# Hybrid flow step, one core: the first loads in another order, six conditioning units in the output projection, gates ahead of the first features

## The chip, the cores and the metric

The kernel runs on one core of one Trainium2 chip. What counts is the device time of one execution in microseconds (us). Engines are named as the profile names them: PE (matmul), PEld (weight load), DVE (vector), ACT (scalar), POOL (GpSimd), SP (the queue that issues all DMAs of this kernel).

## The reference, cut to what matters

640 tokens (512 latent, 128 context) of 1024 channels go through two layers. Each layer is scaled, shifted and gated by six vectors that come from the conditioning vectors `c` and `c_ctx`:

```python
mod_ctx = silu(c_ctx) @ w_mod[l] + b_mod[l]          # (6 * 1024)
mod_lat = silu(c) @ w_mod[l] + b_mod[l]
sh1, sc1, g1, sh2, sc2, g2 = split(mod, 6)
h = rmsnorm(x, ln1) * (1 + sc1) + sh1
a_qkv, a_z, a_beta, a_alpha, b_q, b_k, b_v, c_q, c_k, c_v, gates = split_cols(h @ w_in)
ya = gated_delta_net(conv_silu(a_qkv), sigmoid(a_beta), softplus(a_alpha), ...)   # mixer A
yb, yc = global_attention(...), window_attention(...)                             # mixers B, C
merged = sig(ga) * (ya @ w_br_a) + sig(gb) * (yb @ w_br_b) + sig(gc) * (yc @ w_br_c)
x = x + g1 * (merged @ w_o)                           # output projection
h2 = rmsnorm(x, ln2) * (1 + sc2) + sh2
x = x + g2 * (relu(h2 @ w_ff1) ** 2 @ w_ff2)
```

## The kernel before, in words

Data lie with channels on the 128 partitions and tokens along the row; the 640 tokens are worked on in two halves of 320. Every product of 32-bit numbers is made as three products of a rounded part (`hi`) and a rest (`lo`).

**Conditioning units.** `w_mod` of a layer is cut into 12 units of 512 columns (2 MB of weights each). Units 0 and 1 give `sh1`, 2 and 3 `sc1`, 4 and 5 `g1`, 6 and 7 `sh2`, 8 and 9 `sc2`, 10 and 11 `g2`. For layer 0 `mod_unit` (L248) makes a unit on PE with the raw 32-bit weights:

```python
for k0 in range(0, KC, nk):
    raw = (pl or fl).tile([P, nk, 512], F32, name="fraw", tag="fraw", bufs=bufs)
    nc.sync.dma_start(out=raw, in_=d["w_mod"][l, :, u, k0:k0 + nk])
    for k in range(k0, k0 + nk):
        for i in range(4):
            PE.matmul(ps[32 * i:32 * i + 32], lhsT=csil[:, 2 * k:2 * k + 32], rhs=raw[:, k - k0, i * P:(i + 1) * P], ...)
mod_finish(l, u, ps)
```

`mod_finish` copies the sums (ACT, L235), turns them with one PE transpose (L237), adds `b_mod` (DVE, L239), and for units 2, 3, 8, 9 makes the norm's scale `A` (DVE, L243). Units 0 to 3 run at the start with six buffers of 512 KB (two k each). The others run with eight loads of 256 KB and three buffers (`FR = 3`), which they share with the weights of the filling work. Layer 1's units are made on DVE during the MLP of layer 0 (`mod_sum`); the change leaves them.

**Norm and projection.** `norm` (L282) squares `x` on ACT, adds on DVE (L293), sums over partitions with small matmuls (L298), takes the power -0.5 on POOL, spreads it with small matmuls (L306), and then makes for each of eight k `x * A * rstd` (DVE, L312), plus `sh` (ACT, L314, tile `hh`) and the rest (DVE, L315).

**Mixer A and the filling work.** The projections of mixers B and C and of the branch gates are 36 units (`unit`, L412, matmuls L422) of 48 matmuls. They are recorded at low priority, and a scheduler places them between the instructions of mixer A (gated DeltaNet, "GDN") and of the attention. Mixer A's features are made by `gdn_feat` (L387: matmuls L189, convolution on DVE L405); its per-token gates (L440 to L514) from a projection with 32 matmuls (L451), a copy, a chain of small DVE and ACT instructions, and small matmuls (L490 to L493). `gdn_prep` (L518) transposes the features (L528), normalises them (DVE L542), transposes again (L546) and multiplies by the decay made from the gates (L556 to L561). Conditioning units 4 to 7 stand in the list of the filling work, one behind every eighth unit (`MS = 8`). Filling matmuls are also paced by SP (L201).

**Output projection** (L1115 to L1130, matmuls L189 on `mh`/`ml` and `ghi`/`glo`): eight column blocks j for the first half of the tokens, then eight for the second; `resid` adds to `x`. Units 8 to 11 are recorded behind blocks 0, 2, 4, 6 of the first half. Then the norm's second half and the MLP (L1132 on).

**Order.** Each engine works through its instructions in the order that the scheduler fixed when the program was built. A DMA waits on SP for its buffer, and also until the DMA eight before it has landed: the framework gives the DMAs eight completion semaphores in turn.

Of the kernel before, what the change touches and what calls it, by code (L numbers as in the profile page):

```python
# [9 lines left out]
F32 = mybir.dt.float32  # L10
# [7 lines left out]
P = 128  # L18
# [3 lines left out]
HALF = 320  # L22
DEPTH = 2
DFF = 4096
KC = 8
# [5 lines left out]
M_GDN, M_BND, M_N = 0, 192, 448  # L31
# [39 lines left out]
def weave(*gens):  # L71
    active = list(gens)
    while active:
        live = False
        for g in list(active):
            try:
                live |= next(g) is None
            except StopIteration:
                active.remove(g)
        if not live:  # L80
            return
# [3 lines left out]
MB, FM, FB, FR, OFF = 3, 2, 2, 3, 30000  # L85
PACE, PG = 4, 2
HK = (2, 4, 5)
MS, MP = 8, 0
WRING = 6


# [1 line left out]
def kernel(ctx: ExitStack, tc: tile.TileContext, d: dict):  # L93
    nc = tc.nc
    PE, ACT, DVE, POOL = nc.tensor, nc.scalar, nc.vector, nc.gpsimd

    def pool(name, side="left", bufs=1):
        return tc.tile_pool(name=name, bufs=bufs, side=side, reuse_waits="tile")

    cp = ctx.enter_context(tc.tile_pool(name="cp", bufs=1))  # L100
    psum, turn = {}, {}

    def psum_open(key, name, side, **tags):
        stk = ExitStack()
        pl = stk.enter_context(tc.tile_pool(name=name, bufs=1, space=bass.MemoryType.PSUM, side=side,
                                            reuse_waits="tile"))
        psum[key] = (stk, pl, tags)

    def psum_close(*keys):
        for k in keys:  # L110
            psum.pop(k)[0].close()

    def psum_phase(name, **tags):
        psum_close(*[k for k in ("main",) if k in psum])
        psum_open("main", name, "left", **tags)
# [6 lines left out]
    def bank(shape, tag="m", dt=F32):  # L122
        use = [v for v in psum.values() if tag in v[2]]
        turn[tag] = turn.get(tag, 0) + 1
        _, pl, tags = use[turn[tag] % len(use)]
        return pl.tile(shape, dt, name=tag, tag=tag, bufs=tags[tag])
# [5 lines left out]
    MUL, ADD, SUB = ALU.mult, ALU.add, ALU.subtract  # L132


    cst = cp.tile([P, C_N], F32, name="cst")
    nc.sync.dma_start(out=cst, in_=d["cst"])
    ident = cst[:, C_ID:C_ID + P]
# [13 lines left out]
    hx = ctx.enter_context(pool("hx", "left"))  # L151
    istk = ExitStack()
    npool = istk.enter_context(pool("in0", "left"))
    mraw = npool.tile([P, M_N], F32, name="mraw")
    nc.sync.dma_start(out=mraw, in_=d["msk"])
    mskb = cp.tile([P, 3, 64], BF16, name="mskb")
    DVE.tensor_copy(mskb, mraw[:, M_GDN:M_GDN + 192].rearrange("p (d i) -> p d i", d=3))
    bandb = cp.tile([P, 2, P], BF16, name="bandb")
    DVE.tensor_copy(bandb, mraw[:, M_BND:M_BND + 256].rearrange("p (d i) -> p d i", d=2))
    ones1 = cp.tile([P, 1], F32, name="ones1")  # L160
    DVE.memset(ones1, 1.0)
    mhalf = cp.tile([P, 16], F32, name="mhalf")
# [7 lines left out]
    def load_w(src, pl, bufs, tag="w", rb=2, lo_eng=None):  # L170
        shape = [P, src.shape[1], src.shape[2]]
        raw = pl.tile(shape, F32, name=tag + "raw", tag=tag + "raw", bufs=rb)
        hi = pl.tile(shape, F32R, name=tag + "hi", tag=tag + "hi", bufs=bufs)
        lo = pl.tile(shape, F32R, name=tag + "lo", tag=tag + "lo", bufs=bufs)
        nc.sync.dma_start(out=raw, in_=src)
        split(hi, lo, raw, lo_eng or POOL)
        return hi, lo

    def wcols(w, n, a=0, b=P):
        return [w[0][:, k, a:b] for k in range(n)], [w[1][:, k, a:b] for k in range(n)]  # L180
# [28 lines left out]
        ACT.activation(out, in_, AF.Tanh, scale=0.5)  # L209


    cc = cp.tile([P, KC, 2], F32, name="cc")
    nc.sync.dma_start(out=cc, in_=d["cc"])
    cth = cp.tile([P, KC, 2], F32, name="cth")
    tanh_half(cth, cc)
    csil = cp.tile([P, 2 * KC + 30], F32, name="csil")
# [15 lines left out]
    def mod_finish(l, u, ps):  # L232
        L = lay[l]
        sb = fl.tile([P, P], F32, name="modsb", tag="modsb", bufs=1)
        ACT.copy(sb, ps)  # L235
        pt = bank([P, 4, 32], "fm")
        PE.transpose(pt.rearrange("p i r -> p (i r)"), sb, ident)  # L237
        s = slice(4 * u, 4 * u + 4)
        tt(out=L["mod"][:, s], in0=pt[:, :, 0:2], in1=bc(L["b_mod"][:, s], 2, 2), op=ADD)  # L239
        for n, o in ((0, 8), (1, 32)):  # L240
            if o <= 4 * u < o + 8:
                ks = slice(4 * u - o, 4 * u - o + 4)
                stt(out=L["A"][:, n, ks], in0=L["mod"][:, s], scalar=1.0, in1=bc(L["ln"][:, n, ks], 2, 2),  # L243
                    op0=ADD, op1=MUL)
        if 16 <= 4 * u < 24:
            ts(out=L["g1h"][:, 4 * u - 16:4 * u - 12], in0=L["mod"][:, s], scalar1=0.5, scalar2=None, op0=MUL)

    def mod_unit(l, u, pl=None, nk=1, bufs=FR):  # L248
        ps = bank([P, P], "fm")
# [5 lines that stand above are left out]
                    PE.matmul(ps[32 * i:32 * i + 32], lhsT=csil[:, 2 * k:2 * k + 32], rhs=raw[:, k - k0, i * P:(i + 1) * P],  # L255
                              start=(k == 0), stop=(k == KC - 1), tile_position=(0, 32 * i))
        mod_finish(l, u, ps)
# [64 lines left out]
    xpool = ExitStack()  # L322
    xp = xpool.enter_context(pool("xp0", "right"))
    x = xp.tile([P, KC, NT], F32, name="x")
    for half in range(2):
        s = slice(half * HALF, half * HALF + HALF)
        nc.sync.dma_start(out=x[:, :, s], in_=d["xT"][:, :, s])

    def load_params(l, names):
        shapes = {"b_mod": [P, 48], "ln": [P, 2, KC], "rows": [P, R_N], "conv": [P, 12, 5], "an": [P, 1]}  # L330
        for n in names:
            lay[l][n] = cp.tile(shapes[n], F32, name=f"{n}{l}", tag=n, bufs=1 if n == "rows" else 2)
            nc.sync.dma_start(out=lay[l][n], in_=d[n][l])
# [6 lines left out]
    for l in range(DEPTH):  # L340
        L = lay[l]
        if l == 0:
            load_params(0, ("b_mod", "ln", "rows", "conv", "an"))
            load_params(1, ("b_mod", "ln"))
            psum_phase("ps_in", gm=4)
            for u in range(4):
                mod_unit(0, u, npool, 2, 6)
            istk.close()
        mods = [(mod_unit, l, u) for u in range(4, 8)] if l == 0 else []
        with tc.high_priority(offset=-OFF):  # L350
            for f, *a in mods[:MP]:
                f(*a)
# [23 lines left out]
        def gtile(shape, tag, dt=F32):  # L376
            return (gp if tag in G_EARLY else gdl).tile(shape, dt, name=tag, tag=tag, bufs=GB.get(tag, 1))
# [9 lines left out]
        def gdn_feat(hp, sk):  # L387
            for i in range(3):
                cb = gtile([P, 646], "cb")
                for a, b in ((0, 2), (514, 516), (644, 646)):  # L390
                    POOL.memset(cb[:, a:b], 0.0)
                w = wcols(load_w(d["w_fm"][l, hp * 3 + i], gp, WB), KC)
                for half in range(2):
                    ps = gemm_fm(w, hh, hl, half, TF)
                    if half == 0:
                        ACT.copy(cb[:, 2:322], ps)
                    else:
                        ACT.copy(cb[:, 322:514], ps[:, 0:192])
                        ACT.copy(cb[:, 516:644], ps[:, 192:320])
                yield  # L400
                acc = sk[:, i]
                ci = (4 + hp, hp, 8 + hp)[i]
                ACT.mul(acc, cb[:, 0:642], L["conv"][:, ci, 0:1])
                for j in range(1, 5):
                    stt(out=acc, in0=cb[:, j:j + 642], scalar=L["conv"][:, ci, j:j + 1], in1=acc, op0=MUL, op1=ADD)  # L405
                yield
                th = gtile([P, 642], "so")
                tanh_half(th, acc)
                stt(out=acc, in0=th, scalar=1.0, in1=acc, op0=ADD, op1=MUL)
                yield  # L410
# [23 lines left out]
        fills = [(unit, u) for u in U_ORDER + tuple(range(12, 36))]  # L434
        fills = [f for i in range(36) for f in fills[i:i + 1] + mods[i // MS:i // MS + 1] * (i % MS == MS - 1)]

        sk = gtile([P, 3, 642], "sk")
        weave(gdn_feat(0, sk))

        ba = gtile([P, 5, 32], "ba")  # L440
        wraw = gtile([P, KC, 32], "wraw")
        wba = gtile([P, KC, 2, 32], "whi", F32R)
# [3 lines left out]
        for half in range(2):  # L446
            s = slice(half * HALF, half * HALF + HALF)
# [65 lines left out]
        egs = gtile([P, 2, 5, 8], "egs")  # L513
        ACT.activation(egs.rearrange("p c t h -> p c (t h)"), gs, AF.Exp)  # L514

        cnt, busy, dbusy = [0, 0], {}, {}

        def gdn_prep(hp, t, sk, stg, out):  # L518
# [290 lines left out]
        for hp in range(3):  # L809
            nprep, ndab, nz = {}, [], {}  # L810
            sk = gtile([P, 3, 642], "sk")
# [287 lines left out]
        x = xp.tile([P, KC, NT], F32, name="x")  # L1099
# [17 lines left out]
        nrm = norm(l, 1, 0, x, h2h, h2l, sc)  # L1117
        for j in range(KC):
            resid(j, 0, gemm_fm(ws[j], mh, ml, 0), L["g1h"])
            if l == 0 and j in (0, 2, 4, 6):  # L1120
                mod_unit(0, {0: 8, 2: 9, 4: 10, 6: 11}[j])
        again = KC - WRING
        order = [*range(again, KC), *range(again)]
        for i, j in enumerate(order):
# [7 lines left out]
        with pool(f"ff{l}", "left") as fp:  # L1132
            mods = [(1, u) for u in range(12)] if l == 0 else []
# [165 lines left out]
    for half in range(2):  # L1299
        s = slice(half * HALF, half * HALF + HALF)  # L1300
# [104 lines left out]
```

## Time and profile before

| what | value |
|---|---|
| time, median of 3 runs (lowest, highest) | 2769.16 us (2767.98, 2770.24) |
| profiled execution: its time, its span | 2765.79 us, 2764.0 us |
| PE busy | 2631.6 us (95%) |
| DVE busy | 1989.5 us (72%) |
| ACT busy, POOL busy | 1262.2 us (46%), 977.6 us (35%) |
| DMA share, mean rate | 29.6% of 16 engines, 97 GB/s |

The span runs from the first to the last instruction that the profiler saw; the time of the same execution is 1.79 us longer. Busy time of PE counts matmuls that overlap their neighbours' ends, so a busy PE may still run at the lower of its two clock levels; the granted clock ("PEclk") is a column of its own.

### The profile page before, as it was taken

The page shows a single profiled execution, that of the slowest core. Times are in us where ns is not written, and L with a number is a line of the kernel's source. Part 1 is how long each engine was busy: PE and PEld are TensorE (multiplying, and loading weights), DVE is VectorE, ACT ScalarE, POOL GpSimd, SP SyncE. Part 2 cuts the span into 40 slices and gives each one's busy share as a digit, 9 for nine tenths or more (in the row PEclk, how much of TensorE's full clock was granted, in tenths as well). Part 3 has the DMA queues.
Part 4 walks back from the last instruction along what each step waited for, and adds up shares of the span by engine and source line. Part 5 has one row for each costly group of instructions (what it writes and reads, how often), then busy time and mean ns, then how long its engine had stood idle before and what let it go on. Part 6 is the DMA issues. An engine that isn't in the chain of part 4 may idle for free. (4 is left out here: it accounts for less than half of the span.)

```text
span 2764.0 us, 55264 instructions
## 1 busy us (share of the span) xinstructions
PE 2631.6 (95%) x20820; PEld 2454.3 (89%) x20820; DVE 1989.5 (72%) x4245; ACT 1262.2 (46%) x3054; POOL 977.6 (35%) x1269
## 2 busy tenths in 40 slices
PE   6989999999999999999999999999999999999999
PEld 4878888998888899999988888889998789999999
DVE  4788887555567478999966888875556676676564
ACT  3435545555544243444344355455555444343341
POOL 2534543463454011122125445444645530121110
PEclk8999999999999999999999999999999999999999
DMA  6231112232325523555422211112323241222221
GB/s 228 74 100 43 58 48 71 96 123 93 97 88 189 185 80 109 152 156 154 148 82 86 76 53 53 56 45 97 103 70 114 76 162 62 72 90 70 70 99 61
DMA packets 117017, 268.60 MB, mean 97 GB/s; under 512 B 13584, under 2 KB 22416, under 8 KB 116752
## 3 DMA queue, kind: packets, MB, share of 16 engines
q1 hardware_dynamic: 116752, 265.08, 29.6%
q8 instruction: 165, 2.70, 0.4%
q14 instruction: 100, 0.82, 0.1%
HBM read 232.52 MB, written 32.51 MB: 96 GB/s over the span
## 5 line engine op out<-in xcount | busy, mean ns | idle before, releaser
L422 PE MATMUL fm<-hh,fhi 128*128 128x320 f32 x2304 | 445.3, 325 | 18.9 <-ACT hh L314 8.3
L422 PEld LDWEIGHTS fm<-hh,fhi 128*128 128x128 f32 x2304 | 359.7, 194 | 32.2 <-ACT hh L314 11.3
L168 POOL TENSOR_TENSOR rl<-fr,rh 128x320 fp32r<-128x320 f32 x128 | 142.1, 1115 | 673.5 <-ACT rh L167 673.5
L168 POOL TENSOR_TENSOR flo<-fraw,fhi 128x512 fp32r<-128x512 f32 x176 | 240.0, 1365 | 248.2 <-ACT fhi L167 155.2
L167 ACT CAST ghi<-graw 128x1024 fp32r<-128x1024 f32 (+1 forms) x148 | 144.9, 980 | 225.5 <-PE gm L1259 129.9
L422 PE MATMUL fm<-hh,flo 128*128 128x320 f32 x1152 | 235.4, 324 | 9.2 <-SPq L201 9.1
L1106 DVE SCALAR_TENSOR_TENSOR x<-gm,mod,x 128x320 f32<-128x320 f32 (+2 forms) x384 | 153.9, 431 | 83.9 <-PE gm L1259 83.0
L168 DVE TENSOR_TENSOR glo<-graw,ghi 128x1024 fp32r<-128x1024 f32 (+1 forms) x148 | 171.5, 1160 | 35.7 <-ACT ghi L167 20.2
L1259 PE MATMUL gm<-rl,ghi 128*128 128x320 f32 x1024 | 196.6, 310 | 0.0
L1259 PE MATMUL gm<-rh,ghi 128*128 128x320 f32 x1024 | 195.1, 310 | 1.3 <-DVE x L1106 1.3
L422 PEld LDWEIGHTS fm<-hh,flo 128*128 128x128 f32 x1152 | 181.6, 193 | 16.6 <-SPq L201 10.4
L1259 PE MATMUL gm<-rh,glo 128*128 128x320 f32 x1024 | 192.0, 309 | 0.0
L167 ACT CAST fhi<-fraw 128x512 fp32r<-128x512 f32 x192 | 119.1, 620 | 148.8 <-PE fm L422 62.9
L189 PE MATMUL mb<-hh,whi 128*128 128x320 f32 x1024 | 169.9, 313 | 4.4 <-ACT whi L167 4.4
L1259 PEld LDWEIGHTS gm<-rh,ghi 128*128 128x128 f32 x1024 | 161.0, 188 | 2.7 <-issue 2.4
L1259 PEld LDWEIGHTS gm<-rl,ghi 128*128 128x128 f32 x1024 | 161.7, 188 | 1.0 <-issue 1.0
L1259 PEld LDWEIGHTS gm<-rh,glo 128*128 128x128 f32 x1024 | 160.8, 188 | 0.0
L189 PEld LDWEIGHTS mb<-hh,whi 128*128 128x128 f32 x1024 | 152.8, 188 | 7.3 <-ACT whi L167 5.3
L597 DVE TENSOR_TENSOR stmp<-sv 128x31 f32<-128x31 f32 (+15 forms) x248 | 131.0, 528 | 6.1
L270 DVE SCALAR_TENSOR_TENSOR macc<-fraw,csil,macc 128x512 f32<-128x512 f32 x168 | 133.9, 814 | 0.0
L1197 PE MATMUL gm<-hh,ghi 128*128 128x320 f32 x768 | 130.2, 310 | 0.0
L977 ACT ACTIVATE p<-s,nb 128x640 f32<-128x640 f32 (+3 forms) x160 | 103.0, 648 | 51.2 <-PE pt L1007 24.9
(330 smaller groups left out, 6325.2 us busy)
## 6 DMA issues: line engine op xcount, KB each, us to landing
graw<-w_ff SPq DMA_DIRECT2D x128, 512.0 KB, 3.3
fraw<-w_mod SPq DMA_DIRECT2D x160, 256.0 KB, 2.9
fraw<-w_fm SPq DMA_DIRECT2D x144, 256.0 KB, 2.8
f_spill<-fgt SPq DMA_DIRECT2D x72, 320.0 KB, 2.2
wraw<-w_fm SPq DMA_DIRECT2D x32, 512.0 KB, 3.4
gts<-f_spill SPq DMA_DIRECT2D x48, 320.0 KB, 3.1
fraw<-w_br SPq DMA_DIRECT2D x48, 256.0 KB, 2.8
graw<-w_o SPq DMA_DIRECT2D x20, 512.0 KB, 4.7
```

The costliest lines, as they stand in the source:

```text
L167: ACT.copy(hi, src)
L168: (lo_eng or DVE).tensor_tensor(out=lo, in0=src, in1=hi.bitcast(F32), op=SUB)
L189: mm = PE.matmul(ps, lhsT=w_[k], rhs=x_[:, k, s], start=(i == 0 and k == 0), stop=(i == 2 and k == n - 1))
L270: stt(out=a, in0=raw, scalar=c, in1=a, op0=MUL, op1=ADD)
L422: mm = PE.matmul(ps[half], lhsT=w[:, k], rhs=x_[:, 4 * q + k, s], start=(q == 0 and k == 0 and w is hi and x_ is hh), stop=(q == 1 and k = ...
L597: tt(out=tv, in0=bc(W[:, s + 1:32, s], 2, m), in1=bc(XX[:, s, 0:m], 1, n), op=MUL)
L977: ACT.activation(pw, pv, AF.Exp, bias=nb[:, h:h + 1], scale=0.125, accum_out=den[:, h:h + 1])
L1106: stt(out=x[:, j, a:b], in0=ps[:, a - t0:b - t0], scalar=gate[:, j, c:c + 1], in1=x[:, j, a:b], op0=MUL, op1=ADD)
L1197: PE.matmul(ps, lhsT=w_[:, 4 * q + k], rhs=x_[o][:, k], start=(first and i == 0 and k == 0), stop=(i == 2 and k == 3), skip_group_check=True)
L1259: PE.matmul(ps, lhsT=w_[k], rhs=r[k // 2][o][:, k % 2, half_of(half)], start=(i == 0 and k == 0), stop=(i == 2 and k == 3))
```

## The change

Five edits, and all line numbers behind them move up by one to four:

```
-MS, MP = 8, 0
+MS, MP = 14, 0
...
+    cc = cp.tile([P, KC, 2], F32, name="cc")
+    nc.sync.dma_start(out=cc, in_=d["cc"])
     cst = cp.tile([P, C_N], F32, name="cst")
     nc.sync.dma_start(out=cst, in_=d["cst"])
...
-    for half in range(2):
-        s = slice(half * HALF, half * HALF + HALF)
-        nc.sync.dma_start(out=x[:, :, s], in_=d["xT"][:, :, s])
...
         if l == 0:
-            load_params(0, ("b_mod", "ln", "rows", "conv", "an"))
-            load_params(1, ("b_mod", "ln"))
             psum_phase("ps_in", gm=4)
+            load_params(0, ("b_mod", "ln"))
             for u in range(4):
                 mod_unit(0, u, npool, 2, 6)
+                if u < 2:
+                    s = slice(u * HALF, u * HALF + HALF)
+                    nc.sync.dma_start(out=x[:, :, s], in_=d["xT"][:, :, s])
+            load_params(0, ("rows", "conv", "an"))
+            load_params(1, ("b_mod", "ln"))
+            mraw = npool.tile([P, M_N], F32, name="mraw")
+            nc.sync.dma_start(out=mraw, in_=d["msk"])
+            DVE.tensor_copy(mskb, mraw[:, M_GDN:M_GDN + 192].rearrange("p (d i) -> p d i", d=3))
+            DVE.tensor_copy(bandb, mraw[:, M_BND:M_BND + 256].rearrange("p (d i) -> p d i", d=2))
             istk.close()
-        mods = [(mod_unit, l, u) for u in range(4, 8)] if l == 0 else []
+        mods = [(mod_unit, l, u) for u in range(4, 6)] if l == 0 else []
...
-        sk = gtile([P, 3, 642], "sk")
-        weave(gdn_feat(0, sk))
...
+        sk = gtile([P, 3, 642], "sk")
+        weave(gdn_feat(0, sk))
...
             resid(j, 0, gemm_fm(ws[j], mh, ml, 0), L["g1h"])
-            if l == 0 and j in (0, 2, 4, 6):
-                mod_unit(0, {0: 8, 2: 9, 4: 10, 6: 11}[j])
+            if l == 0 and j in (0, 1, 2, 3, 4, 5):
+                mod_unit(0, {0: 6, 1: 7, 2: 8, 3: 9, 4: 10, 5: 11}[j])
```

The number of PE matmuls in the built program is the same, 17,706. Where they stand differs; three places follow. A row is an instruction or a run of equal ones; in the changed kernel `mod_unit`'s load and matmul are L248 and L251, its transpose L233, the norm's matmuls L294 and L302, `gemm_fm`'s L187, the gates' L448, L453 and L487 on.

SP, the program's first rows, before: (`fraw<-w_mod` is a load of a conditioning unit, `xT` the input, `msk` the masks, the rest parameters)

```order
L136 DMA cst<-cst 128x740
L155 DMA mraw<-msk 128x448
L213 DMA cc<-cc 128x16
L327 DMA x<-xT 128x8x320 x2
L333 DMA b_mod_118<-b_mod 128x48
L333 DMA ln_120<-ln 128x16
L333 DMA rows_122<-rows 128x296
L333 DMA conv_124<-conv 128x60
L333 DMA an_126<-an 128x1
L333 DMA b_mod_128<-b_mod 128x48
L333 DMA ln_130<-ln 128x16
L252 DMA fraw<-w_mod 128x1024 x6
```

and of the changed kernel:

```order
L136 DMA cc<-cc 128x16
L138 DMA cst<-cst 128x740
L325 DMA b_mod_115<-b_mod 128x48
L325 DMA ln_117<-ln 128x16
L248 DMA fraw<-w_mod 128x1024 x4
L341 DMA x<-xT 128x8x320
L248 DMA fraw<-w_mod 128x1024 x2
L341 DMA x<-xT 128x8x320
L248 DMA fraw<-w_mod 128x1024
L325 DMA rows_307<-rows 128x296
L325 DMA conv_309<-conv 128x60
L248 DMA fraw<-w_mod 128x1024
```

The first weight is the fifth load instead of the thirteenth; seven small loads and the masks' load stand among the weights of units 1 and 2 (the fence ends in them).

PE, around the gates of layer 0, before: (`mb` on L189 are features, `fm` on L422 filling work, L451 and L456 the gates' projection and its transposes, L528 `gdn_prep`)

```order
L189 MATMUL mb<-hh,whi 128x320
L189 MATMUL mb<-hh,wlo 128x320 x8
L422 MATMUL fm<-hh,flo 128x320
L422 MATMUL fm<-hh,fhi 128x320 x4
L451 MATMUL mb<-hh,whi 64x320 x32
L528 MATMUL mb<-cst,sk 128x128 x2
L422 MATMUL fm<-hh,fhi 128x320 x4
L422 MATMUL fm<-hh,flo 128x320
L456 MATMUL ma<-cst,zz 128x32 x2
```

and of the changed kernel:

```order
L422 MATMUL fm<-hh,fhi 128x320 x8
L448 MATMUL mb<-hh,whi 64x320 x32
L422 MATMUL fm<-hh,flo 128x320 x4
L422 MATMUL fm<-hh,fhi 128x320 x3
L453 MATMUL ma<-cst,zz 128x32 x2
L422 MATMUL fm<-hh,fhi 128x320
L453 MATMUL ma<-cst,zz 128x32 x3
L422 MATMUL fm<-hh,fhi 128x320 x4
L187 MATMUL mb<-hh,whi 128x320 x28
```

The gates' 32 matmuls stand in the second filling unit, behind its first eight matmuls and ahead of the first feature matmul, instead of behind the last feature.

PE, the end of the output projection's second half and the norm behind it, before: (`hh` at the end is the MLP's first block)

```order
L189 MATMUL gm<-mh,glo 128x320 x8
L298 MATMUL gm<-ones_85,nacc 64x1
L298 MATMUL gm<-ones_85,nacc 128x1 x2
L306 MATMUL gm<-cst,nrstd 128x64
L306 MATMUL gm<-cst,nrstd 128x128 x2
L189 MATMUL gm<-hh,ghi 128x320 x16
```

and of the changed kernel:

```order
L187 MATMUL gm<-mh,glo 128x320 x8
L233 MATMUL fm<-cst,modsb 128x128
L251 MATMUL fm<-fraw,csil 32x128 x16
L294 MATMUL gm<-ones_83,nacc 64x1
L294 MATMUL gm<-ones_83,nacc 128x1 x2
L251 MATMUL fm<-fraw,csil 32x128 x8
L302 MATMUL gm<-cst,nrstd 128x64
L302 MATMUL gm<-cst,nrstd 128x128 x2
L187 MATMUL gm<-hh,ghi 128x320 x16
```

Six of the last unit's eight groups of four matmuls stand between the last block and the norm's two small products.

## Rows read from the trace of the kernel before

**Rows 1.** The page's first part: busy us (share of the span) and instructions.

```profile
PE 2631.6 (95%) x20820; PEld 2454.3 (89%) x20820; DVE 1989.5 (72%) x4245; ACT 1262.2 (46%) x3054; POOL 977.6 (35%) x1269
```

**Rows 2.** Timeline of SP from the start: start us, us, engine, line, transfer.

```profile
2.11 1.37 SPq L327 DMA_DIRECT2D x<-xT  x2
...
13.05 2.89 SPq L252 DMA_DIRECT2D fraw<-w_mod  x6
```

**Rows 3.** Waits of SP in 0 to 60 us: total us, times, longest.

```profile
SPq L252 <- DMA x<-xT: 3.3, 1, 3.3
```

**Rows 4.** Windows: stretch, length, busy us by engine, PEclk, DMA share, GB/s.

```profile
2.00:12.00 10.00, 0.00 (x0) 0.00 (x0) 2.62 (x10) 2.39 (x7) 0.00 (x0) 1.00 0.99 329
12.00:14.00 2.00, 0.00 (x0) 0.00 (x0) 1.56 (x4) 1.84 (x5) 0.00 (x0) 1.00 0.42 83
14.00:22.00 8.00, 6.38 (x56) 5.05 (x60) 3.87 (x11) 2.99 (x7) 1.04 (x1) 1.00 1.01 383
22.00:24.00 2.00, 2.00 (x34) 1.31 (x26) 0.28 (x3) 0.00 (x0) 0.39 (x1) 1.00 0.57 163
24.00:40.00 16.00, 11.53 (x170) 8.01 (x169) 1.49 (x6) 2.27 (x6) 2.97 (x3) 0.78 1.02 400
```

**Rows 5.** Timeline of DVE, 38 to 60 us.

```profile
38.98 0.17 DVE L243 SCALAR_TENSOR_TENSOR A<-mod,ln 128x8 f32<-128x8 f32 x1
...
43.91 0.17 DVE L243 SCALAR_TENSOR_TENSOR A<-mod,ln 128x8 f32<-128x8 f32 x1
...
57.80 1.03 DVE L315 SCALAR_TENSOR_TENSOR hh<-ntmp,mod,hh 128x128 fp32r<-128x128 f32 x3
```

**Rows 6.** Waits of PE in 150 to 200, 400 to 450 and 540 to 700 us.

```profile
PE fm L255 <- DMA fraw<-w_mod: 3.4, 3, 1.6
...
PE fm L255 <- DMA fraw<-w_mod: 1.8, 1, 1.8
...
PE fm L255 <- DMA fraw<-w_mod: 2.8, 5, 1.2
```

**Rows 7.** Windows around units 4 to 7, the end of attention, the output projection.

```profile
190.00:204.00 14.00, 10.63 (x111) 8.13 (x110) 5.99 (x9) 6.08 (x18) 5.03 (x18) 0.88 0.57 180
424.00:442.00 18.00, 16.20 (x173) 11.68 (x173) 11.96 (x35) 9.37 (x32) 7.70 (x14) 0.81 0.53 156
556.00:570.00 14.00, 12.58 (x141) 9.85 (x140) 4.37 (x10) 5.56 (x17) 9.16 (x13) 0.76 0.65 209
670.00:684.00 14.00, 12.63 (x153) 9.42 (x152) 8.80 (x19) 6.68 (x17) 8.23 (x13) 1.00 0.67 207
900.00:966.00 66.00, 66.00 (x597) 56.10 (x596) 29.09 (x61) 18.14 (x33) 4.98 (x5) 1.00 0.57 180
...
856.00:868.00 12.00, 9.44 (x93) 6.78 (x92) 9.23 (x36) 6.60 (x25) 3.28 (x6) 1.00 0.23 67
```

**Rows 8.** The loads of L252 in 880 to 966 us: issue to landing.

```profile
DMA to landing us min/median/max: 2.6/3.1/5.7
```

**Rows 9.** Timeline of PE in the output projection: a unit's matmuls, three runs of blocks'.

```profile
908.71 0.64 PE L255 MATMUL fm<-fraw,csil 128*32 128x128 f32 x16
909.28 0.71 PE L189 MATMUL gm<-mh,ghi 128*128 128x320 f32 x3
909.83 1.33 PE L189 MATMUL gm<-ml,ghi 128*128 128x320 f32 x8
911.00 1.33 PE L189 MATMUL gm<-mh,glo 128*128 128x320 f32 x8
```

**Rows 10.** Waits of PE in 840 to 1010 us.

```profile
PE gm L298 <- DVE nacc L293: 2.9, 1, 2.9
...
PE gm L306 <- POOL nrstd L206: 1.3, 1, 1.3
```

**Rows 11.** Waits of PE in 100 to 130 us, then in 1480 to 1530 us.

```profile
PE mb L546 <- DVE tm L542: 2.5, 2, 1.4
...
PE mb L546 <- DVE tm L542: 2.6, 2, 1.6
```

More of the change, by code (lines that the diff above doesn't have):

```diff
@@ L153 @@
     npool = istk.enter_context(pool("in0", "left"))
-    mraw = npool.tile([P, M_N], F32, name="mraw")
-    nc.sync.dma_start(out=mraw, in_=d["msk"])
     mskb = cp.tile([P, 3, 64], BF16, name="mskb")
-    DVE.tensor_copy(mskb, mraw[:, M_GDN:M_GDN + 192].rearrange("p (d i) -> p d i", d=3))
     bandb = cp.tile([P, 2, P], BF16, name="bandb")
-    DVE.tensor_copy(bandb, mraw[:, M_BND:M_BND + 256].rearrange("p (d i) -> p d i", d=2))
     ones1 = cp.tile([P, 1], F32, name="ones1")
@@ L209, in tanh_half @@
         ACT.activation(out, in_, AF.Tanh, scale=0.5)
-    cc = cp.tile([P, KC, 2], F32, name="cc")
-    nc.sync.dma_start(out=cc, in_=d["cc"])
     cth = cp.tile([P, KC, 2], F32, name="cth")
```

## The prediction, made blind

> **What bounds the kernel now.** I read the page's first part: PE is busy for 2631.6 of 2764.0 us, every other engine for far less [rows 1]. The program has 17,706 matmuls before and after, so the change can only move time in which PE waits, or in which PE works at the lower clock. I therefore went through the stretches that the change touches: SP's timeline and waits at the start, with the rate of the DMAs; PE's waits and granted clock around each conditioning unit that stands in the filling work; the output projection; PE's waits on mixer A's gates. In each the reader is to see what PE waits for, and for how long.
>
> At the start PE waits for the stream of loads. `x` is issued at 2.11 us, but the first weight of a conditioning unit only at 13.05 us [rows 2], held for 3.3 us by `x` [rows 3], since the DMA eight before it must have landed. The windows show the hole that this leaves: 12 to 14 us runs at a share of 0.42, and 22 to 24 us at 0.57; between them the DMAs are full, at 329 GB/s while `x` comes and at 400 GB/s later on weights [rows 4]. The last unit's scale `A` is made at 43.91 us; behind it DVE makes the norm's rows without a break, until 57.80 + 1.03 = 58.83 us [rows 5]. Only then has PE more work than it can do. So the start costs the end of the stream plus a fixed DVE chain of 14.75 us.
>
> The sum is made against the profiled execution: 2764.0 us of span and 1.79 around it, 2765.79 us. The median of the runs is 3.37 us above that; I add this to the end.
>
> **The first loads, -4.3 us (bounds -6.2 and -1.7).** From 2 to 40 us the DMAs moved 3.29 + 0.17 + 3.06 + 0.33 + 6.40 = 13.25 MB [rows 4]. In the new order two loads of `w_fm` (0.26 MB each, from their shape) fall behind the last unit's weights, so 12.73 MB precede its end. The weights now start with the fifth load and nothing but their own buffers and the loads eight before hold them, so the two holes should close. With 3.29 MB at 329 GB/s (10 us) and the other 9.44 MB at 400 (23.6 us) the stream ends at 2 + 33.6 = 35.6 us instead of 40: -4.4, less a tenth for the small loads. All at 400 would end at 33.8: -6.2. If both holes come back (2 x 0.58 + 2 x 0.43 = 2.0 us) and one `w_fm` comes ahead after all (0.6), -1.7 is left; these two are the bounds. The casts of the masks on DVE now wait for a load behind units 1 and 2, ahead of the second half's norm sum; they land some 10 us before unit 2's `A`, so they cost nothing unless the stream is late there (this is in the lower bound).
>
> **Two units out of the filling work, -8.2 us (bounds -10.3 and -4.0).** Units 4 to 7 made PE wait 3.4, 1.8 and (two together) 2.8 us for their weights, 8.0 in all [rows 6]; that is 2.0 for a unit. Around three of them the granted clock falls below 1: 0.88 over 14 us, 0.81 over 18, 0.76 over 14, and 1.00 around the fourth [rows 7]. Length times what is missing from 1: 1.7 + 3.4 + 3.4 + 0 = 8.5 us lost, 2.1 for a unit. Two units stay in the filling work, behind the 14th and the 28th filling unit, and two leave: 2 x 4.1 = 8.2. If the dear ones stay away, the two left over save 3.4 + 1.7 + 1.8 + 3.4 = 10.3; if only the waits go and the clock falls elsewhere, 4.0. The matmuls of a unit only move: 8 of them (16 records, each of these 32-bit matmuls is recorded twice) take 0.57 us from start to start [rows 9], 32 take 2.3.
>
> **Less filling work at the end of attention, +1.1 us (bounds 0 and +2.6).** Two units' 2 x 2.6 us (2.3 and a transpose of 0.27) of filler are gone there. From 856 to 868 us PE is idle for 2.56 of 12 us, 21% [rows 7], so a fifth of the 5.2 us of filler may have been cover: 1.1. None, if other filling work takes its place; half, if the idle share is that of a gap that a unit would have filled.
>
> **Six units in the output projection, -0.7 us (bounds -1.7 and +4.1).** Today's four cost no wait: 66.00 of 66.00 us busy at clock 1.00 [rows 7]. A unit brings eight loads into a ring of three buffers, so a load must land while PE does what stands between the release of its buffer and its next use. A load takes 2.6 to 5.7 us, median 3.1 [rows 8], and its issue 0.3. A run of eight block matmuls takes 911.00 - 909.83 = 1.17 us [rows 9]. Counted by that in PE's order, the shortest stretch between a release and the next use holds 4.2 us of work, in both kernels, apart from the last unit. So I take no new stall for five of the six. The last unit's 24 matmuls (1.7 us) stand between the last block and the norm's two small products, where PE waits 2.9 and 1.3 us anyway for DVE and POOL [rows 10]: -1.7. But the run of 16 needs four loads of three buffers; the fourth is released some 0.4 us after the run begins and lands 3.1 + 0.3 later, near 3.9 us, 1.0 behind the end of the 2.9 wait: +1.0. Of the bounds, one takes this loss as nothing, the other lets one whole unit stall like those in the filling work (4.1).
>
> **Gates first, in both layers, -2.6 us (bounds -5.1 and +3.1).** PE waits 2.5 us in layer 0 and 2.6 in layer 1 at L546 for DVE's normalised features [rows 11]. In the old order the gates' chain on DVE comes in the same stretch as these; now it runs while PE multiplies the features. DVE has its share of the features' convolution to do as well, so I take half of 5.1. On the other side the gates' weights are now the next thing that PE needs after the norm; one load that is late costs a landing of 3.1 [rows 8].
>
> **Sum:** -4.3 - 8.2 + 1.1 - 0.7 - 2.6 = -14.7, so 2765.79 - 14.7 = 2751.1 us for a profiled execution, and **2754.5** for the median. All terms at their best give -23.3 (2745.9), at their worst +4.1 (2773.3).
>
> **Rivals.** *The stream gains nothing:* each small load among the weights takes a place among the eight, so that a weight waits for the landing of one that was issued late; the holes only move. For it: SP was held not only by `x`. Against: a hole of 2 us is needed for each one now there. Time 2754.5 + 4.3 = 2758.8.
>
> *Slower, the six units stall in the output projection.* Place: the first half's blocks 0 to 5 and the norm behind them. Each unit pays there what it paid in the filling work, 2.0 of wait and 2.1 of clock, 6 x 4.1 = 24.6 us, none of which the four cost today: 2754.5 + 24.6 = 2779. It decides from the point where issue and landing together pass the 4.2 us of work between uses. For it: a landing of 5.7 has been seen [rows 8], and half as many units again ask for weights in the same stretch. Against: the median is 3.1, and the DMA share there is 0.57. The Trainium skill ("TensorE: Matmul & The Clock Gate", HAM oscillation) speaks for this rival: bursts of matmuls that are shorter than the wait for the next load lose the clock each time, not once. By that rule a unit's bursts of 0.57 us would lose it wherever they wait for a load; the granted clock agrees for three of the four units in the filling work, and in the output projection, where nothing waits, it is 1.00 [rows 7].
>
> *More than the terms:* the gates' waits go wholly, and the dear pair of units is the one removed: -2.5 and -2.1 on top, with the stream at its best (-1.9): about 2748.
>
> *The scheduler gives it back:* with other work at hand, the order of mixer A's instructions changes in all of 100 to 840 us, and new waits for DVE there cost some 10 us, as much as twice both waits of rows 11: 2764.5.
>
> **Chances.** Forecast 0.50 (2750 to 2758), no gain from the stream 0.17, more than the terms 0.15, order gives it back 0.10, stall in the output projection 0.08. The range is 2744 to 2767: it leaves out the stall and a little at either end. A change of 0.2% (5.5 us) is about what a measurement of this kernel can tell from none; faster is below 2763.6. The forecast, the first and the third rival are faster: 0.79 with a little taken off for luck near the bound. Same holds the fourth rival and what is taken off, 0.13; slower 0.08.
>
> **What would show it.** First loads: the first weight is issued before 4 us, no window before 36 us has a share under 0.9, unit 3's `A` is made near 39.5 us, and the norm ends near 54.5. Units: PE waits for `w_mod` near 4 us in all between 100 and 840 us, with two dips of the clock instead of three. Output projection: no wait on `w_mod` but one near 1 us behind the last block, clock 1.00. Gates: the waits of the second transposes (L546, now near L545) come to 2.6 us in both layers together, and no wait of the gates' matmuls on their weights. The prediction is wrong if `A` stays near 44 us, if the clock dips as often with two units as with four, or if the features, now later by the gates' 32 matmuls, make mixer A wait elsewhere.

## The result, and the profile after

| | before | changed | ratio (95% interval) |
|---|---|---|---|
| first runs, 4 of each | 2768.57 us | 2753.38 us (2752.26 to 2756.94) | 0.995 (0.9934 to 0.9965) |
| more runs, 17 and 6 | 2767.05 us | 2756.87 us (2754.87 to 2762.11) | 0.996 (0.9946 to 0.9974) |

The change saves 15 us by the first runs and 10 by the later ones, where 14.7 was forecast. The profiled execution of the changed kernel took 2756.94 us, 8.9 less than the one of before; a second one took 2757.18. PE's part of the page, which answers to [rows 1]:

```profile
PE 2625.6 (95%) x20820; PEld 2454.2 (89%) x20820; DVE 1994.3 (72%) x4245; ACT 1265.9 (46%) x3054; POOL 983.8 (36%) x1269
```

**The start.** The windows of the changed kernel (columns as in [rows 4]):

```profile
2.00:12.00 10.00, 3.38 (x52) 1.99 (x56) 0.70 (x5) 0.21 (x1) 0.00 (x0) 1.00 0.94 317
12.00:14.00 2.00, 1.42 (x17) 0.64 (x15) 0.16 (x1) 0.27 (x1) 0.00 (x0) 1.00 1.09 380
14.00:22.00 8.00, 3.48 (x38) 2.47 (x38) 3.71 (x11) 3.94 (x10) 0.00 (x0) 1.00 1.06 383
22.00:24.00 2.00, 0.98 (x4) 0.93 (x4) 1.35 (x4) 1.68 (x5) 0.86 (x1) 1.00 1.03 368
24.00:36.00 12.00, 10.33 (x114) 7.39 (x112) 3.03 (x11) 3.24 (x8) 3.35 (x3) 1.00 0.98 345
36.00:40.00 4.00, 3.61 (x65) 2.16 (x64) 3.33 (x9) 1.68 (x4) 0.00 (x0) 1.00 0.89 348
```

The two holes are closed: 12 to 14 us runs at a share of 1.09, 22 to 24 at 1.03. But from 24 us on a full share moves only 345 GB/s, where it moved 400. By 24 us 7.73 MB have come instead of 6.85, by 40 us 13.26 instead of 13.25. DVE, which answers to [rows 5], then ACT from 42 us:

```profile
36.46 0.17 DVE L239 SCALAR_TENSOR_TENSOR A<-mod,ln 128x8 f32<-128x8 f32 x1
...
41.24 0.17 DVE L239 SCALAR_TENSOR_TENSOR A<-mod,ln 128x8 f32<-128x8 f32 x1
...
56.08 1.02 DVE L311 SCALAR_TENSOR_TENSOR hh<-ntmp,mod,hh 128x128 fp32r<-128x128 f32 x3
```

```profile
42.33 0.30 ACT L709 COPY H<-Hs 64x128 f32<-64x128 f32 x1 [1.71 <-DMA Hs<-state]
42.64 0.29 ACT L710 COPY H<-Hs 64x128 f32<-64x128 f32 x1
42.96 1.01 ACT L310 ACTIVATE hh<-ntmp,mod 128x320 fp32r<-128x320 f32 x2
```

Unit 3's `A` comes 2.67 us earlier (41.24 for 43.91), the norm's end only 1.73 (57.10 for 58.83). In between ACT stands 1.71 us in front of a copy of the state `H`, whose load has not landed; the norm's `hh` is queued behind it on ACT, and DVE waits for that, 0.9 us longer than elsewhere. Before, the same copies had their data in time.

**The filling work and mixer A.** PE's waits from 60 us to the output projection, first of the changed kernel (to 883 us), then of the kernel before (to 900 us), rows that differ much:

```profile
PE fm L422 <- ACT fgt L207: 4.0, 1, 4.0
PE fm L422 <- ACT fgt L429: 3.8, 1, 3.8
PE mb L187 <- ACT whi L165: 3.3, 3, 1.6
...
PE fm L422 <- SPq L199: 2.9, 5, 1.2
PE fm L422 <- POOL flo L166: 2.7, 2, 1.4
PE fm L251 <- DMA fraw<-w_mod: 2.5, 3, 1.1
```

```profile
PE fm L422 <- SPq L201: 8.0, 4, 3.2
PE fm L255 <- DMA fraw<-w_mod: 8.0, 9, 1.8
...
PE mb L189 <- ACT whi L167: 1.6, 1, 1.6
...
PE fm L422 <- ACT fgt L209: 1.0, 1, 1.0
```

The waits on the units' weights fell by 5.5 us and those on SP's pacing by 5.1, but the three waits on ACT grew, by 3.0, 3.8 and 1.7 (1.0, none and 1.6 before), and one on POOL, by 2.7 (none before). The windows of these stretches show what that amounts to (before, then changed):

```profile
60.00:900.00 840.00, 796.49 (x6777) 717.62 (x6776) 594.70 (x1344) 416.08 (x1119) 396.79 (x534) 0.98 0.29 92
```

```profile
60.00:883.00 823.00, 781.28 (x6635) 711.71 (x6634) 597.39 (x1339) 415.90 (x1113) 399.18 (x534) 0.98 0.27 87
```

PE's idle time is 840.00 - 796.49 = 43.5 us before and 41.7 after: all but 1.8 us of the wait that left came back under other names. The first block of the output projection starts at 883.6 instead of 900.3 us.

**The output projection.** PE at its end (answers to [rows 10]):

```profile
961.16 1.08 PE L251 MATMUL fm<-fraw,csil 128*32 128x128 f32 x24
965.59 0.66 PE L251 MATMUL fm<-fraw,csil 128*32 128x128 f32 x8 [3.35 <-DMA fraw<-w_mod]
966.17 1.31 PE L294 MATMUL gm<-ones,nacc 128*64 128x1 f32 x6
967.42 1.08 PE L251 MATMUL fm<-fraw,csil 128*32 128x128 f32 x16
968.79 1.83 PE L302 MATMUL gm<-cst,nrstd 64*128 64x64 f32 x6 [0.29 <-POOL nrstd L204]
970.28 4.61 PE L187 MATMUL gm<-hh,ghi 128*128 128x320 f32 x16
```

The norm's sum no longer waits for DVE: PE stands 3.35 us for the last unit's weights first. From the first block to the MLP's first matmul it takes 970.3 - 883.6 = 86.7 us, before 980.7 - 900.3 = 80.4. Two more units are 5.1 us of matmuls, but the last unit's final eight (0.6 us) and its transpose (0.27) stand behind the MLP's first matmul here, and none did before. So of the 6.3 more, 4.3 are matmuls that moved here, and 2.0 are lost.

**The gates.** PE's waits in 100 to 130 us, then in 1480 to 1530 (answers to [rows 11]):

```profile
PE mb L527 <- DVE sk L409: 1.4, 1, 1.4
PE mb L545 <- DVE tm L541: 1.2, 2, 0.6
```

```profile
PE mb L545 <- DVE tm L541: 1.3, 2, 0.7
PE mb L527 <- DVE sk L409: 1.2, 1, 1.2
```

2.6 and 2.5 us, as before; half of it now stands one step earlier, at the transposes of the features (L527), which come later. The chain of the gates on DVE is over at 88.7 us in the changed kernel. DVE's rows ahead of the two waits at L545 in 100 to 130 us:

```profile
122.78 0.43 DVE L541 TENSOR_TENSOR tm<-tm,grs 128x256 f32<-128x256 f32 x1 [0.96 <-POOL grs L204]
125.51 1.50 DVE L541 TENSOR_TENSOR tm<-tm,grs 128x256 f32<-128x256 f32 x1 [2.30 <-POOL grs L204]
```

DVE itself stands idle there for POOL's power of -0.5, and the second row takes 1.50 us where the first takes 0.43.

### The profile page after: what moved, and what is told of

Same layout as the page of the kernel before. It is cut to its first block, busy times and chain, and to the rows that moved or that the text cites. A ratio compares the mean times of both kernels' runs of the same rounds, so it can differ in the third digit from the quotient of the medians.

```text
span 2755.2 us, 55267 instructions
## 1 busy us (share of the span) xinstructions
PE 2625.6 (95%) x20820; PEld 2454.2 (89%) x20820; DVE 1994.3 (72%) x4245; ACT 1265.9 (46%) x3054; POOL 983.8 (36%) x1269
## 5 line engine op out<-in xcount | busy, mean ns | idle before, releaser
L422 PE MATMUL fm<-hh,fhi 128*128 128x320 f32 x2304 | 449.7, 325 | 30.3 <-ACT hh L310 8.9
L422 PEld LDWEIGHTS fm<-hh,fhi 128*128 128x128 f32 x2304 | 357.6, 193 | 47.5 <-ACT hh L310 11.8
L422 PE MATMUL fm<-hh,flo 128*128 128x320 f32 x1152 | 233.2, 323 | 6.8 <-POOL flo L166 4.2
L166 DVE TENSOR_TENSOR glo<-graw,ghi 128x1024 fp32r<-128x1024 f32 (+1 forms) x148 | 171.0, 1156 | 34.8 <-ACT ghi L165 19.6
L422 PEld LDWEIGHTS fm<-hh,flo 128*128 128x128 f32 x1152 | 181.6, 192 | 13.7 <-POOL flo L166 5.0
L187 PE MATMUL mb<-hh,whi 128*128 128x320 f32 x1024 | 171.1, 315 | 6.0 <-ACT whi L165 5.6
L187 PEld LDWEIGHTS mb<-hh,whi 128*128 128x128 f32 x1024 | 153.6, 189 | 9.3 <-ACT whi L165 6.8
L1196 PE MATMUL gm<-hh,ghi 128*128 128x320 f32 x768 | 130.2, 310 | 0.0
```

Source lines behind the costliest of these rows:

```text
L166: (lo_eng or DVE).tensor_tensor(out=lo, in0=src, in1=hi.bitcast(F32), op=SUB)
L187: mm = PE.matmul(ps, lhsT=w_[k], rhs=x_[:, k, s], start=(i == 0 and k == 0), stop=(i == 2 and k == n - 1))
L422: mm = PE.matmul(ps[half], lhsT=w[:, k], rhs=x_[:, 4 * q + k, s], start=(q == 0 and k == 0 and w is hi and x_ is hh), stop=(q == 1 and k = ...
L1196: PE.matmul(ps, lhsT=w_[:, 4 * q + k], rhs=x_[o][:, k], start=(first and i == 0 and k == 0), stop=(i == 2 and k == 3), skip_group_check=True)
```

## The experiments

Kernels in one group ran beside the kernel before on the same chip; a ratio is to that. Its 28 and 28 runs in the first two groups had medians of 2765.34 and 2766.67 us.

**The parts alone.** The first group undid the change down to one part, and once the gates alone. Loads alone is the changed kernel with these lines back:

```
-MS, MP = 14, 0
+MS, MP = 8, 0
...
-        mods = [(mod_unit, l, u) for u in range(4, 6)] if l == 0 else []
+        mods = [(mod_unit, l, u) for u in range(4, 8)] if l == 0 else []
...
-            if l == 0 and j in (0, 1, 2, 3, 4, 5):
-                mod_unit(0, {0: 6, 1: 7, 2: 8, 3: 9, 4: 10, 5: 11}[j])
+            if l == 0 and j in (0, 2, 4, 6):
+                mod_unit(0, {0: 8, 2: 9, 4: 10, 6: 11}[j])
```

and the features' two lines ahead of the gates again. Expected:

> The kernel before with the new order of the first loads alone. By the terms of the prediction: 4.3 us below the kernel before, the norm's last row of DVE near 54.5 us. By the traces of before and after: the norm's end moves from 58.83 only to 57.1 us, so 1.7 us below before. By the rival that the order of all later instructions decides: the start still gives 1.7, but the time lies anywhere within 6 us of before, and the difference arises between 60 and 900 us.

Measured: 2763.77 us, ratio 0.9995 (0.9986 to 1.0003), so 1.4 us saved, between 3.9 and a loss of 0.8. `A` is made at 43.08 us and the norm ends at 58.03, 0.83 and 0.80 us earlier than before. No copy of `H` waits here, and the chain behind `A` takes 14.78 us, as forecast. The stream is what gains so little: from 24 to 36 us it moves 307 GB/s at a share of 0.95. The term of 4.3 is too large.

Units alone is the kernel before with the diff above turned round.

> The kernel before with only the units moved (two in the filling work, six in the output projection). By the terms: 8.2 - 1.1 + 0.7 = 7.8 us below before. By the traces of the two kernels, where nearly all of the gain lies between 58 and 884 us and the output projection loses: 8 to 12 us below, the first matmul of the output projection about 15 us earlier (5.1 us of it matmuls that moved), and the MLP behind it 9 earlier. By the rival that the order decides: less than 4 us below, with new waits of other kinds between 100 and 840 us.

Measured: 2758.12 us, ratio 0.997 (0.9959 to 0.9981), 8.3 us saved (5.2 to 11.3). Its window from 60 us to the output projection:

```profile
60.00:881.00 821.00, 777.64 (x6649) 708.42 (x6648) 594.74 (x1341) 416.16 (x1116) 396.65 (x534) 0.99 0.27 89
```

Idle 43.4 us, as before (43.5), though the waits on `w_mod` fell from 8.0 to 2.7. What fell in this pair of profiles is the time at the lower clock. Summed over windows of 10 us (10 us times what is missing from 1), it is 20.4 us before and 10.2 here. From the norm's end to the first block it takes 19.2 us less: 5.1 moved, 10.2 are clock, 0.1 is idle time, and 3.8 are in none of these. Three such windows of the kernel before, then the same of this one:

```profile
180.00:190.00 10.00, 8.30 (x47) 8.30 (x48) 9.33 (x26) 3.64 (x10) 2.86 (x7) 0.83 0.19 61
190.00:200.00 10.00, 6.63 (x77) 4.63 (x75) 4.37 (x5) 3.67 (x12) 2.75 (x12) 0.84 0.60 193
...
430.00:440.00 10.00, 8.96 (x102) 6.73 (x103) 4.82 (x11) 4.44 (x17) 4.88 (x8) 0.66 0.51 154
```

```profile
180.00:190.00 10.00, 6.26 (x43) 6.03 (x44) 9.54 (x20) 3.75 (x10) 4.18 (x8) 1.00 0.22 80
190.00:200.00 10.00, 10.00 (x72) 9.79 (x71) 6.20 (x11) 5.78 (x17) 4.77 (x12) 1.00 0.25 86
...
430.00:440.00 10.00, 10.00 (x149) 7.88 (x149) 7.77 (x24) 7.25 (x24) 4.78 (x7) 1.00 0.09 29
```

It has dips of its own elsewhere, 0.70 from 400 us and 0.67 from 720, away from its two units. One pair of profiles does not fix the clock's part: summed in the same way, the four kernels with four units of loads in the filling work (before, loads alone, gates alone, and the changed kernel without the units) lose 18.8 to 20.5 us with 43.5 to 46.5 us idle, and six profiles of kernels with two lose 10.2 to 18.7 with 39.2 to 45.4 idle. By the means, 19.6 and 13.9, the clock gives about 5.7.

The gates alone, the kernel before with this:

```
-        sk = gtile([P, 3, 642], "sk")
-        weave(gdn_feat(0, sk))
         ba = gtile([P, 5, 32], "ba")
...
+        sk = gtile([P, 3, 642], "sk")
+        weave(gdn_feat(0, sk))
         cnt, busy, dbusy = [0, 0], {}, {}
```

> The kernel before with only the gates ahead of the first features, in both layers. By the terms: 2.6 us below before. By the traces, where the waits of the second transposes stay (2.2 and 3.1 us after, 2.5 and 2.6 before): within 1.5 us of before. By the rival that the order decides: up to 5 us to either side, with the difference in other waits of the gated DeltaNet.

Measured: 2766.50 us, ratio 0.9998 (0.9988 to 1.0008): 0.6 us saved, between 3.3 and a loss of 2.2. Its waits at L527 and L545 are 1.4 and 1.1 us in 100 to 130 us, 1.6 and 2.2 in 1480 to 1530: not less than [rows 11]. The last of the group is the changed kernel with that diff turned round:

> The changed kernel with the gates put back behind the first features; loads and units as changed. By the terms: 2.6 us above the changed kernel, 12.1 below before. By the traces: the same time as the changed kernel within 1.5 us. If the parts do not add up (order decides), it differs from the sum of loads alone and units alone by more than 3 us.

Measured: 2752.81 us, ratio 0.9954 (0.9942 to 0.9966), the changed kernel's time with the old order of the gates. The gates' new place gives nothing that can be measured.

**What a unit costs in the filling work.** The kernel before, with units 4 to 7 made by

```
+    def mod_unit_r(l, u):
+        ps = bank([P, P], "fm")
+        for k in range(KC):
+            for i in range(4):
+                PE.matmul(ps[32 * i:32 * i + 32], lhsT=csil[:, 2 * k:2 * k + 32], rhs=cst[:, i * P:(i + 1) * P],
+                          start=(k == 0), stop=(k == KC - 1), tile_position=(0, 32 * i))
+        mod_finish(l, u, ps)
...
-        mods = [(mod_unit, l, u) for u in range(4, 8)] if l == 0 else []
+        mods = [(mod_unit_r, l, u) for u in range(4, 8)] if l == 0 else []
```

> The kernel before, but units 4 to 7 in the filling work multiply constants that lie in the buffer of constants already, so that their 32 loads are left out (their results are then not those of the reference) while all matmuls stay. By the prediction's terms the waits of 8.0 us and the 8.5 us of clock go: 16.5 us below before. If the wait only moves to other names (between 60 us and the output projection PE idles for 43.5 us before and 41.7 after the change, though 5.5 us of waits on these weights are gone): only the clock is gained, 4 to 9 us below before, with the same idle time. If neither waits nor clock matter and the moved matmuls alone gave the gain: within 2 us of before.

Measured: 2749.21 us, ratio 0.9944 (0.9932 to 0.9956), 15.5 us saved (12.2 to 18.8), where 16.5 stood in the terms: 3.9 for a unit instead of 4.1. Here the idle time falls too:

```profile
60.00:879.00 819.00, 782.51 (x6772) 710.16 (x6771) 592.14 (x1342) 416.00 (x1117) 394.30 (x534) 0.99 0.26 83
```

36.5 us idle, 7.0 less, and 8.5 us lost to the clock, 11.9 less. Not only the loads differ: without them the scheduler placed the units elsewhere, their first matmuls at 191, 404, 545 and 653 us instead of 191, 424, 557 and 672. The run does not separate the loads from the order. The same exchange for the two units that are left in the changed kernel:

> The changed kernel, but its two units in the filling work multiply constants that lie there already; 16 loads are left out and these units' results are not the reference's. If every unit in the filling work costs what the four of the kernel before cost (15.5 us by four): 7.8 us below the changed kernel. By the waits that are left on these loads in the changed kernel's trace (2.5 us) and its clock: 2.5 to 6 us below.

Measured: 2756.79 us, ratio 0.9957 (0.9945 to 0.997), beside 0.996 of the changed kernel in the same group: no difference that these runs can tell, whose intervals are some 3.5 us to either side. The waits on `w_mod` are gone, and three others have grown (the changed kernel's second profile has 3.1, 3.0 and 2.4 us for them):

```profile
PE fm L187 <- ACT yhl L165: 8.9, 4, 4.4
PE mb L553 <- DVE tm L549: 5.7, 6, 1.4
...
PE ma L642 <- POOL dbd L627: 4.9, 2, 2.7
```

So the 3.9 us are a mean over four units in one exchange, which also changed the order, not a price that each further unit brings.

**The output projection.** Its six units from constants, 48 loads left out:

```
-                mod_unit(0, {0: 6, 1: 7, 2: 8, 3: 9, 4: 10, 5: 11}[j])
+                mod_unit_r(0, {0: 6, 1: 7, 2: 8, 3: 9, 4: 10, 5: 11}[j])
```

> The changed kernel, but the six units of the output projection multiply constants that lie there already; 48 loads are left out and these units' results are not the reference's. By the prediction (no stall but one behind the last block): 0 to 3 us below the changed kernel, the wait of 3.3 us on the weights gone and the norm's waits of 2.9 and 1.3 us back. By the rival that six units stall there as in the filling work: 20 us or more below.

Measured: 2751.50 us, ratio 0.9936 (0.9924 to 0.9949), 5.4 us below the changed kernel and more than the 0 to 3 expected, though the intervals reach down to that. Without loads the scheduler puts these matmuls from 842 us on, in the end of attention, and PE's idle time ahead of the output projection falls to 39.2 us; the wait of 3.3 on weights is gone, those of 3.3 and 1.3 on the norm are back. The rival of 20 us or more is out. Six buffers of their own for the six units:

```
-                mod_unit(0, {0: 6, 1: 7, 2: 8, 3: 9, 4: 10, 5: 11}[j])
+                mod_unit(0, {0: 6, 1: 7, 2: 8, 3: 9, 4: 10, 5: 11}[j], mp, 1, 6)
```

> The changed kernel, but the six units in the output projection take their weights through a ring of their own with six buffers of 256 KB. If the ring of three is what makes PE wait behind the last block: that wait of 3.3 us is gone, the waits on the norm's sum and power (2.9 and 1.3 us before) are back, and the time is 0 to 3 us below the changed kernel, since the last unit's matmuls then find other places. If loads collide instead (w_o, x and w_ff behind the units' loads): waits of blocks on their weights appear and the time is above the changed kernel.

Measured: 2761.13 us, ratio 0.9984 (0.9975 to 0.9992), slower than the changed kernel. Its waits in 840 to 1010 us:

```profile
PE gm L294 <- DVE nacc L289: 3.3, 1, 3.3
PE fm L251 <- DMA fraw<-w_mod: 1.6, 2, 1.4
...
PE gm L302 <- POOL nrstd L204: 1.3, 1, 1.3
```

The wait behind the last block changed hands once more, and a load now takes 4.7 us (median), 3.3 with three buffers. These three rows come to 6.2 us, where the changed kernel waits 3.6 (3.3 and 0.3). Why the run saves 5 to 10 us less than the changed kernel is open, since the two profiled executions differ by 0.8. All eight units there, with three buffers and then with six:

```
-        mods = [(mod_unit, l, u) for u in range(4, 6)] if l == 0 else []
+        mods = [(mod_unit, l, u) for u in range(4, 4)] if l == 0 else []
...
+        if l == 0:
+            mod_unit(0, 4)
         for j in range(KC):
...
-            if l == 0 and j in (0, 1, 2, 3, 4, 5):
-                mod_unit(0, {0: 6, 1: 7, 2: 8, 3: 9, 4: 10, 5: 11}[j])
+            if l == 0 and j < 7:
+                mod_unit(0, j + 5)
```

> The changed kernel with all eight units 4 to 11 in the output projection (unit 4 ahead of block 0, unit 5 to 11 behind blocks 0 to 6) and none in the filling work. If a unit costs 4.1 us in the filling work and next to nothing in the output projection, as the prediction has it: 7 us below the changed kernel. If the ring of three buffers is full with six units (the changed kernel's trace shows a wait of 3.3 us for a load behind the last block): the waits on weights between 850 and 1000 us grow to 8 us or more and the time is that of the changed kernel or up to 6 us above it.

> All eight units in the output projection and six buffers for them. If a unit's 4.1 us in the filling work are its load's wait and the clock that falls with it, and only the ring limits the output projection: 6 to 10 us below the changed kernel (2743 to 2747 beside a kernel before at 2765). If the gain of the moved units came from a luckier order: within 4 us of the changed kernel to either side.

Measured: 2758.70 us, ratio 0.9973 (0.9964 to 0.9981), and 2757.81, 0.9971 (0.9959 to 0.9983). With three buffers PE waits 5.9 us for weights, and three units run into the MLP's first block; from the MLP's first matmul (L187) to the first of the next products (L1196, L1198 there) it takes 98.0 us instead of 88.5, of which 5.1 are matmuls that moved there. Neither beats the changed kernel: the 7 us that two more units promised are not there, as with the two units made from constants. Ahead of the run the kernel with six buffers was put within 4 us of the changed kernel if the moved units had gained by a luckier order; it saves 8.9 us beside the later runs' 10.2. So this rival is not out: a run that takes the loads away and leaves the order of the matmuls as it is would decide, and there is none.

**The changed kernel again, and without the units.** The second is the changed kernel with the first diff of this section.

> The changed kernel itself, with more runs and a second profile, beside the other kernels of this group. By the prediction's sum 14.7 us below the kernel before; by the sum of the parts alone (1.4 + 8.3 + 0.6) 10.3 below; if its first runs were luckier than those of the kernels with other rings: 4 to 8 below.

> The changed kernel with the units back (four in the filling work, four in the output projection), the loads and the gates as changed. By the prediction's terms 4.3 + 2.6 = 6.9 us below the kernel before, 7.8 above the changed one. By the runs of the parts alone: 2.0 us below before (0 to 4), 8 to 12 above the changed one.

Measured: the changed kernel 0.996, as in the table; without the units 2765.58 us, ratio 0.9991 (0.9979 to 1.0003), 2.5 us saved (between 5.8 and a loss of 0.8). Loads and gates together give what they gave alone; the units are the gain.

## Why the prediction was right, step by step

The total was right, and so was the size of the largest term; the terms of the loads and of the gates, and the split of the largest term into waits and clock, were not.

- **First loads (-4.3): mis-sized, -1.7 by the changed kernel's trace, -0.8 by that of loads alone, -1.4 by the runs.** The holes closed as said. The step that failed is the rate: 400 GB/s was taken for all the weights, and a nearly full share moved 345 from 24 to 36 us, or 307 in loads alone. With `A` 2.67 us earlier in the changed kernel, the fixed chain of 14.75 us behind it was not fixed either: the load of the state is now what is late, and the copy that waits for it holds ACT. By this the first rival (the stream gains nothing) came nearer than the forecast on this term; the bound of 1.7 is met by the one trace and missed by the other. Which of the loads lower the rate was not tested.
- **Units (-8.2, with the cover and the output projection -7.8): right in size, -8.3 alone, but not by the way forecast, so in part by luck.** The price of 4.1 a unit was 3.9 where the loads were taken away and the order changed with them. The step that failed is that a wait on weights that goes is time gained: these waits did fall by 5.3 us in units alone, but others took their place and the idle time stayed (43.5 and 43.4). The clock was to give 4.2; it gave 10.2 in one pair of profiles and about 5.7 by the means of all. The price does not hold for the next two units either. That the loads, and not the order, make the gain is argued and not shown.
- **Less filling work (+1.1).** No run takes it by itself; it is in the -8.3.
- **Output projection (-0.7): +2.0, inside its bounds.** The late fourth load is there, at 965.59 - 961.16 = 4.4 us behind the start of the run where 3.9 was said; but it stands alone where the norm's wait was, and the matmuls behind it hide little. The stalls of the rival did not come: no block waits for weights ahead of the last one. The Trainium skill ("TensorE: Matmul & The Clock Gate", HAM oscillation) spoke for that rival: bursts shorter than the wait for their next load lose the clock each time. The filling work agrees only in part: before, the windows from 190, 430 and 560 us, in which units wait for weights, are at 0.84, 0.66 and 0.66; in units alone the two units wait 2.7 us as well, and the windows that hold them (330 to 370 and 590 to 610 us) are at 1.00. In the output projection one such wait is left, and the clock is not at 1.00 there as forecast: 0.73 from 960 to 970 us. Before, behind the norm's waits, it was 0.74 from 980 to 990.
- **Gates (-2.6): nothing.** The step that failed is that the second transposes wait because DVE does the gates' chain. With the chain gone from there DVE is still late, since it waits for POOL's power first (0.96 and 2.30 us), and now it is late for the features (L527) as well.
- **The sum.** Alone the parts give 1.4 + 8.3 + 0.6 = 10.3 us; the changed kernel saves 10 to 15. Whether there is something between the parts cannot be said at this spread. The loads and the gates were to give 6.9 and give 2.0, or 2.5 together; that the first runs still came out near 14.7 is in part luck. The later runs, 10.2 saved, fit the first rival as well (2758.8 us, 10.4 saved).
- **The signs of being wrong.** `A` did move, to 41.24 us, where 39.5 was said. The clock falls below 0.9 in nine windows of 10 us before, in eight in the first profile of the changed kernel and in five in the second; in the first, only the window from 600 us holds one of its two units. So the sign that it dips as often is there in one profile. Mixer A does wait elsewhere, but not for the gates' new place: the two waits of PE on ACT's `fgt` that grew are there in units alone too (4.1 and 3.7 us).

## What to carry to other kernels

Check a wait that is to be removed against the idle time of the whole stretch, not against its own row: on an engine fed by several others the next one that is late takes its place, and only a run without the cause shows the balance. A price worked out from four waits is their mean in one order of the program; the fifth may cost nothing. And a stream of loads should be priced with the rate that it has among its new neighbours.

## What the runs showed of the hardware

One and the same kernel before took 2758.93 to 2775.83 us in 17 runs on one chip, and 2760.31 to 2774.15 in 28 on another. The low clock does not fall in the same places each time: two executions of the changed kernel, with waits that differ by little, show these windows (the first, then the second).

```profile
390.00:400.00 10.00, 5.98 (x51) 5.17 (x50) 9.83 (x12) 4.40 (x15) 6.03 (x10) 0.90 0.08 27
400.00:410.00 10.00, 10.00 (x60) 9.99 (x61) 5.89 (x8) 4.80 (x13) 6.33 (x11) 0.76 0.27 93
...
560.00:570.00 10.00, 9.76 (x67) 8.98 (x68) 4.80 (x8) 3.46 (x8) 5.74 (x4) 0.83 0.33 111
```

```profile
390.00:400.00 10.00, 5.38 (x46) 4.68 (x46) 9.83 (x12) 4.39 (x14) 5.77 (x9) 0.98 0.08 27
400.00:410.00 10.00, 9.83 (x65) 9.63 (x67) 6.79 (x10) 5.63 (x16) 7.19 (x11) 0.84 0.30 97
...
560.00:570.00 10.00, 8.24 (x65) 7.36 (x66) 6.53 (x7) 3.45 (x8) 6.87 (x4) 1.00 0.33 107
```

Over 60 us to the output projection that is 17.0 us lost to the clock in one and 10.4 in the other, for the same program: 6.6 us, where the whole change saves 10 to 15. A clock term read from one profile is uncertain by as much. And it is not time one for one: the two executions took 2756.94 and 2757.18 us, and the second, with less lost to the clock, had PE idle for 45.4 us there instead of 41.7.

Where the clock falls behind a wait, it can cost more than the wait. In the kernel before PE stands still once between 424 and 442 us, for 1.80 us ahead of 431.04, for a unit's weights. In the windows of 2 us from 432 on the granted clock is 0.57, 0.50, 0.50 and 0.73, so PE works at the lower of its two levels for some 7 us and loses 3.4. In units alone a wait of 1.16 us for weights (at 341 us) is followed by a clock of 1.00.
